# A hybrid four-branch block: RWKV's Gram masks moved to VectorE, and a fourth raw weight buffer in place of a branch slot

## The chip, the cores and the metric

The kernel runs on one core of a Trainium2 chip. The metric is the device time of one execution in microseconds (us), median of several runs; lower is better. The core has TensorE (PE: matmuls, with its weight loads shown apart as PEld), VectorE (DVE), ScalarE (ACT), GpSimd (POOL) and SyncE (SP), which issues DMAs. Each engine works through its own instructions in order and waits on semaphores for the others.

## The reference

The input `x` has 256 tokens of 2048 numbers. It is normalised, multiplied by one wide matrix `w_in` (2048 x 21648), and the columns are split among four branches (HGRN2, S5, RWKV-7, Mamba-2), each 1024 wide. Each branch's output is gated, multiplied by its `w_up`, gated again by a sigmoid of more columns of `w_in`, and summed; then come `w_out`, a norm and the residual:

```python
h = rmsnorm(res, norm_pre[l])
(q_a, f_a, i_a, z_a, u_b, z_b, rkvwa_c, z_c, xbc_d, dt_d, z_d,
 gate_pre) = project_partitioned(h, w_in[l], IN_SPLITS)
...
o_c = rwkv7_branch(...) * jax.nn.silu(z_c)
...
contrib = gate * jnp.einsum('blw,wd->bld', outs[b], w_up[l, b].astype(F32))
merged = contrib if merged is None else merged + contrib
...
y = jnp.einsum('bld,de->ble', merged, w_out[l].astype(F32))
res = res + rmsnorm(y, norm_post[l])
```

The change touches the RWKV branch. Its reference is a recurrence over tokens, with 16 heads of a 64 x 64 state:

```python
sa = jnp.einsum('bhvk,bhk->bhv', state, -kk_t)
state = (state * w_t[:, :, None, :]
         + sa[..., None] * (kk_t * a_t)[:, :, None, :]
         + v_t[..., None] * k_t[:, :, None, :])
return state, jnp.einsum('bhvk,bhk->bhv', state, r_t)
```

The kernel computes it in four chunks of 64 tokens. For every head and chunk it forms Gram matrices between tokens (products of r and kk with k and b), and keeps of each only the causal part: either on and above the diagonal or strictly above it. That is where the masks come in.

## The kernel before

All big weights are streamed from HBM in chunks of 512 KB, 444 of them, each a part of a unit (a block of columns of `w_in`, `w_up`, `w_glu` or `w_out`). The class `_Stream` handles them:

- `load` (L1569) issues a chunk's DMA from SP into a tile `raw`, of which there are `RAW_BUFS` = 3 (L56). `loads` runs ahead of the split by `RAW_BUFS - LAG` chunks in the main loop (L1700). A load into a buffer waits until the split of the chunk that had the buffer before has read it.
- `split` (L1581) makes of `raw` a rounded `hi` on ScalarE (L207, the helper `act`) and the rest `lo` on VectorE (L216, the helper `tt`), so that fp32 accuracy comes from three fast matmuls (hi by h, hi by the low part of h, lo by h). There are four pairs of `hi` and `lo` (`HL_BUFS`).
- `products` issues these matmuls (L261, the helper `mm`): 24 a chunk with 256 columns, or 12 with 512, into a PSUM tile `pg`.

Between the chunks the planner `run_jobs` (L1559) puts the branches' work: each branch is a generator whose `yield`s divide it into stages. Each operation is booked on a modelled time of its engine (`t_pe`, `t_act`, `t_dve`, `t_sw` for GpSimd). Stages are started, by priority, while neither VectorE's nor ScalarE's booked time is more than `AHEAD` = 3.0 us ahead of PE's, and when the work that a stage needs should be done. The order of all instructions on all engines is thus fixed when the program is built, and it depends on every booked cost and on the free slots. If a unit needs a branch that isn't done, `finish` issues the rest of its stages at once.

The branches' tiles of 4 KB a partition come from a pool of `NSLOT` = 37 slots (L54); a `raw` tile is of the same size. Some stages ask for room first (`wait`, and the S5 branch's look ahead at L1473). Branches also use four PSUM banks `pb` (`bank`), asked for with `wait_banks`. DMAs of the branches (`ld`, `ldx`) go through GpSimd's queue in the main loop, and stores (`st`) through ScalarE's.

The Gram stage of RWKV (`rwkv_branch`, L531 to L580) does this for each chunk c of 64 tokens: twice, for four groups of two heads, 8 matmuls of `bk` by `L1` into two banks; then four copies on ScalarE out of PSUM, each 64 partitions x 512, two into `L1[c][e]` (L548) and two into `GB[c]` (L549). After both halves, four `affine_select`s on GpSimd (L561, the helper `select`), each over 64 x 1024 in place, zero the part that isn't causal. Of the two 64 x 64 blocks in each, one keeps the diagonal and the other doesn't; which of them is which alternates with c (o = c % 2). Then `GB`'s strict part is stored to the DRAM tensor `dab` (L562) by GpSimd's queue, and `bk` is transposed and copied into `bkT`. In the profile `L1` shows as `L`. Later the blocks of `dab` are inverted on VectorE, and the recurrence over the four chunks runs on `L1`, `GB`, `bkT`. The S5 branch's tiles (scans at L243 among them) and the evacuations of units run in between.

`setup_consts` makes the constants on GpSimd near the start, among them `lmask` (L356) with memsets and `affine_select`s like those that the change adds.

Of the kernel before, what the change touches and what calls it, by code (L numbers as in the profile page):

```python
# [11 lines left out]
F32 = mybir.dt.float32  # L12
F32R = mybir.dt.float32r
I8 = mybir.dt.int8
BF16 = mybir.dt.bfloat16
AF = mybir.ActivationFunctionType
ALU = mybir.AluOpType
# [33 lines left out]
NPAR = 384  # L51


NSLOT = 37  # L54
SLOT = 1024
RAW_BUFS = 3  # L56
LAG = 1
BANKS = 4
BLOCKED = -1
# [14 lines left out]
class _Kern:  # L74


    def __init__(self, ctx, tc, drams):
# [4 lines left out]
        self.wpool = ctx.enter_context(tc.tile_pool(name="wpool", bufs=3))  # L82
        self.slots = ctx.enter_context(tc.tile_pool(name="slots", bufs=NSLOT))
        self.small = ctx.enter_context(tc.tile_pool(name="small", bufs=1))
# [35 lines left out]
    def room(self, n):  # L120
        return self.live(self.tiles) + n <= NSLOT

# [191 lines left out]
def setup_consts(K):  # L314
    nc = K.nc
    d = K.d
    c = K.const
    K.pt = c.tile([128, NPAR], F32, name="pt")
    src = {"norm_pre": d["norm_pre"], "lb": d["hgrn_lb_logits"], "hgrn_norm": d["hgrn_norm"],
           "s5_d": d["s5_d"], "b_glu": d["s5_b_glu"], "w0": d["rwkv_w0"], "a0": d["rwkv_a0"],  # L320
           "k_k": d["rwkv_k_k"], "k_a": d["rwkv_k_a"], "r_k": d["rwkv_r_k"], "ln_w": d["rwkv_ln_w"],
           "ln_b": d["rwkv_ln_b"], "m2_norm": d["m2_norm"], "conv_b": d["m2_conv_b"],
           "mu": d["rwkv_mu"], "conv_w": d["m2_conv_w"], "a_re": d["s5_a_re"], "a_im": d["s5_a_im"]}
    rows = K.big([128, 3, 128], name="prow")
    nc.vector.memset(rows, 0.0)
    for m, n in enumerate(_PAR_ROWS):
        if m in (6, 12):
            yield
        o, r = PAR[n]
        a = src[n][0]  # L330
        if len(a.shape) == 2:
            a = a.rearrange("a b -> (a b)")
        K.ldx(rows[o % 128:o % 128 + r, o // 128, :], a.rearrange("(r p) -> r p", p=128))
    yield
    K.ones = c.tile([128, 1], F32, name="ones")
    nc.gpsimd.memset(K.ones, 1.0)
    K.halfpi = c.tile([128, 1], F32, name="halfpi")
    nc.gpsimd.memset(K.halfpi, HALF_PI)

    K.ind = c.tile([128, 2, 32], F32, name="ind")  # L340
    nc.gpsimd.memset(K.ind, 0.0)
    for e in range(2):
        for g in range(2):
            nc.gpsimd.memset(K.ind[64 * e:64 * e + 64, g, 2 * g + e:2 * g + e + 1], 1.0)
    K.m64 = c.tile([128, 512], BF16, name="m64")
    nc.gpsimd.memset(K.m64, 1.0)
    nc.gpsimd.memset(K.m64[:, 0:512:64], 0.0)
    K.m256 = c.tile([128, 512], BF16, name="m256")
    nc.gpsimd.memset(K.m256, 1.0)
    nc.gpsimd.memset(K.m256[:, 0:512:256], 0.0)  # L350
    K.causal = c.tile([128, 128], F32, name="causal")
    nc.gpsimd.memset(K.causal, 1.0)
    nc.gpsimd.affine_select(out=K.causal, in_=K.causal, pattern=[[1, 128]], base=0, channel_multiplier=-1,
                            compare_op=ALU.is_ge, fill=0.0)

    K.lmask = c.tile([128, 7, 64], I8, name="lmask")  # L356
    nc.gpsimd.memset(K.lmask, 0.0)
    for e in range(2):
        x = slice(64 * e, 64 * e + 64)
        for lv in range(6):  # L360
            h = 1 << lv
            nb = 32 // h
            v = K.lmask[x, lv + 1, :].rearrange("p (b u) -> p b u", u=2 * h)[:, :, h:2 * h]
            nc.gpsimd.memset(v, 1.0)
            nc.gpsimd.affine_select(out=v, in_=v, pattern=[[-2 * h, nb], [0, h]], base=0, channel_multiplier=1,
                                    compare_op=ALU.is_ge, fill=0.0)
            nc.gpsimd.affine_select(out=v, in_=v, pattern=[[2 * h, nb], [0, h]], base=h - 1, channel_multiplier=-1,
                                    compare_op=ALU.is_ge, fill=0.0)
    K.omu = c.tile([128, 25], F32, name="omu")
    yield  # L370
    for e in range(2):
        x = slice(64 * e, 64 * e + 64)
        nc.vector.tensor_copy(out=K.lmask[x, 0, :], in_=K.ident[x, x])
    yield from K.wait_banks(1)
    ps = K.bank()
    for j in range(3):
        K.tr(ps[:, j * 128:(j + 1) * 128], rows[:, j, :])
    nc.vector.tensor_copy(out=K.pt, in_=ps[:, 0:NPAR])
    K.ts(K.omu, K.parv("mu"), -1.0, 1.0, ALU.mult, ALU.add)
# [16 lines left out]
def rwkv_branch(K, rw):  # L396

    nc = K.nc
# [10 lines left out]
    for g in range(2):  # L409
# [3 lines left out]
        for ii in range(4):  # L413
            i = 4 * g + ii
# [3 lines left out]
        for ii in range(4):  # L418
            i = 4 * g + ii
# [23 lines left out]
    ps = K.bank()  # L443
# [34 lines left out]
    ps = K.bank()  # L478
# [4 lines left out]
    b = ic  # L483
# [10 lines left out]
    L1 = [[K.big([128, 8, 2, 64], name=f"L1{c}{e}") for e in range(2)] for c in range(4)]  # L494
    for c in range(4):
        o = c % 2
        s0, s1 = 64 * c, 64 * c + 64
        for e in range(2):
            x = slice(64 * e, 64 * e + 64)
# [12 lines left out]
    for c in range(4):  # L512
# [3 lines left out]
        for e in range(2):  # L516
            x = slice(64 * e, 64 * e + 64)
# [9 lines left out]
    GB, bkT = [], []  # L527
# [3 lines left out]
    for c in range(4):  # L531
        o = c % 2
        GB.append(K.big([128, 8, 2, 64], name=f"GB{c}"))
        bkT.append(K.big([128, 16, 64], name=f"bkT{c}") if c < 3 else None)
        for i4 in range(2):
            yield from K.wait_banks(2)
            ps = [K.bank([128, 4, 128]) for _ in range(2)]
            for ii in range(4):
                i = 4 * i4 + ii
                for e in range(2):  # L540
                    x = slice(64 * e, 64 * e + 64)
                    K.mm(ps[e][:, ii, :], fl2(bk[c][x, i]), fl2(L1[c][e][x, i]))
            yield 1
            for e in range(2):
                x = slice(64 * e, 64 * e + 64)
                y = slice(64 * (1 - e), 64 * (1 - e) + 64)
                i0 = slice(4 * i4, 4 * i4 + 4)
                K.act(L1[c][e][y, i0].rearrange("p i a b -> p i (a b)"), ps[e][y], AF.Copy)  # L548
                K.act(GB[c][x, i0].rearrange("p i a b -> p i (a b)"), ps[e][x], AF.Copy)  # L549
                if e == 0:  # L550
                    yield 0
            del ps
            if i4 == 0:
                yield 0
        pat = [[0, 8], [-1 if o == 0 else 1, 2], [1, 64]]
        base = 0 if o == 0 else -1
        for e in range(2):
            x = slice(64 * e, 64 * e + 64)
            y = slice(64 * (1 - e), 64 * (1 - e) + 64)
            for ap in (GB[c][x], L1[c][e][y]):  # L560
                K.select(ap, pattern=pat, base=base, channel_multiplier=-1, compare_op=ALU.is_ge, fill=0.0)  # L561
            K.ld(dab[c, :, e, :, :].rearrange("i s t -> s i t"), GB[c][x, :, 1 - o, :])  # L562
        if c == 3:
            bk[c] = None
            break

        pt = []
        yield from K.wait_banks(2)
        for e in range(2):
            x = slice(64 * e, 64 * e + 64)  # L570
            ps = K.bank([128, 8, 64])
            pt.append(ps)
            for i in range(8):
                K.tr(ps[:, i, :], fl2(bk[c][x, i]), 64 * e)
        yield 1
        for e in range(2):
            K.act(bkT[c][:, e:16:2, :], pt[e], AF.Copy)
        bk[c] = None
        del pt, ps
        yield 0  # L580
# [10 lines left out]
    for s in range(31):  # L591
        n, m = s + 1, 31 - s
# [29 lines left out]
    for q in range(2):  # L622
        ps = [K.bank([128, 8, 32]) for _ in range(2)]
        zps.append(ps)
        for o in range(2):
            z0 = 64 * (1 - o) + 32
            for h in range(16):
                i, e = h // 2, h % 2
                x = slice(64 * e, 64 * e + 32)
# [12 lines left out]
    for q in range(2):  # L642
        ps = K.bank([128, 16, 32])
# [44 lines left out]
    for q in range(2):  # L688
# [4 lines left out]
        else:  # L693
            for e in range(2):
                x = slice(64 * e, 64 * e + 64)
# [6 lines left out]
        for o in range(2):  # L702
            c = 2 * q + o
# [4 lines left out]
            for h in range(16):  # L708
                i, e = h // 2, h % 2
# [11 lines left out]
            for h in range(16):  # L721
                i, e = h // 2, h % 2
                K.mm(pu[64 * e:64 * e + 64, i, :], TT[q][ab:ab + 64, h, :], R1(e)[:, i, :])
            yield 1
            for e in range(2):
                x = slice(64 * e, 64 * e + 64)
# [3 lines left out]
            if c < 3:  # L730
                yield from K.wait_banks(1)
                pst = K.bank([128, 8, 64])
                for h in range(16):
                    i, e = h // 2, h % 2
                    K.mm(pst[64 * e:64 * e + 64, i, :], bkT[c][:, h, :], wc[e][:, i, 1, :])
            for h in range(16):
                i, e = h // 2, h % 2
                x = slice(64 * e, 64 * e + 64)
# [3 lines left out]
            if c < 3:  # L742
                if o == 1:
                    carry = GB[0][:, :, 0, :]
                for e in range(2):
                    x = slice(64 * e, 64 * e + 64)
# [16 lines left out]
    v = K.fm("v")  # L763
# [3 lines left out]
    for q in range(2):  # L767
        y = Y[q]
# [15 lines left out]
        for g in range(2):  # L784
            yield from K.wait_banks(1)
            ps = K.bank([128, 4, 128])
            for ii in range(4):
                i = 4 * g + ii
                K.tr(ps[:, ii, :], yf[:, i * 128:(i + 1) * 128])
            yield 1  # L790
            for ii in range(4):
                i = 4 * g + ii
# [713 lines left out]
class _Stream:  # L1506
# [62 lines left out]
    def load(self, j):  # L1569
        u, c = self.chunks[j]  # L1570
        K = self.K
        t = K.wpool.tile([128, u.kc, u.nc_], F32, tag="raw", name=f"raw{j}", bufs=RAW_BUFS)
        k0 = c * u.kc * 128
        K.t_sp = max(K.t_sp, self.split_end.pop(j - RAW_BUFS, 0.0))
        soft, K.soft = K.soft, False
# [99 lines left out]
    def prepare(self):  # L1675
# [3 lines left out]
        self.loaded = -1  # L1679
        self.loads(RAW_BUFS)  # L1680

# [4 lines left out]
    def begin(self, j):  # L1686

        self.step = -HL_BUFS
        self.split(j)
        self.loads(j + 1 + RAW_BUFS)  # L1690

# [603 lines left out]
```

## Time and profile before

| | |
|---|---|
| median of 3 runs | 1429.35 us (1428.59 to 1433.24) |
| the profiled execution | 1436.64 us |
| its span, first to last instruction | 1434.9 us |
| moved by DMA | 287.57 MB, mean 200 GB/s |
| raw weight loads | 444 of 512 KB, all from SP |

Times in the trace are microseconds from the start of the span. A group's row reads: line, engine, operation, output <- inputs, shape, count; then busy time, mean duration of one in ns; then the idle time of the engine just before them, and what ended it. A row of windows gives, for each engine, the busy time within the window and the number of instructions, then the granted TensorE clock (1.00 is full speed), the mean busy share of the DMA engines and GB/s. Busy times of matmuls overlap and their ends are modelled, so a busy PE isn't necessarily PE at its peak. The lines themselves stand in the prediction, each beside what it carries.

### The profile page before, as it was taken

How to read it: one execution, taken by the hardware profiler on the slowest of the kernel's cores; microseconds unless marked ns; L12 is line 12 of the kernel's file. 1: busy time of each engine (PE TensorE's matmuls, PEld its weight loads, DVE VectorE, ACT ScalarE, POOL GpSimd, SP SyncE). 2: the span in 40 equal slices, each digit the busy share in tenths (PEclk: the TensorE clock that was granted, in tenths of full speed). 3: DMA queues.
4: the chain of work that ended last, by engine and by line, in shares of the span. 5: the costliest groups of instructions: out<-in, count | busy, mean ns of one | idle time of the engine just before them, and what ended most of it. 6: DMA issues, size and time to landing. Idle time of an engine off the chain costs nothing.

```text
span 1434.9 us, 24425 instructions
## 1 busy us (share of the span) xinstructions
PE 1391.9 (97%) x9623; PEld 1227.7 (86%) x9623; DVE 1059.2 (74%) x1454; ACT 818.6 (57%) x1129; POOL 157.9 (11%) x267
## 2 busy tenths in 40 slices
PE   8998999988999999899999999999999999999997
PEld 7998998988999878798888888887889888888886
DVE  6775976768965757678988779867876798766654
ACT  5465445565437574466357875678647454554442
POOL 6012004133030102100010000000010100000000
PEclk9999999999999999899999999999999999999999
DMA  7775777676797957966678655656585876686564
GB/s 214 210 232 166 217 219 227 184 168 180 227 240 184 223 178 195 238 202 219 194 231 199 190 184 185 202 182 199 178 191 166 205 218 197 195 271 195 182 195 136
DMA packets 198769, 287.57 MB, mean 200 GB/s; under 512 B 12438, under 2 KB 116735, under 8 KB 198655
## 3 DMA queue, kind: packets, MB, share of 16 engines
q1 hardware_dynamic: 169614, 237.15, 54.6%
q0 software_dynamic: 24944, 42.01, 13.9%
q10 hardware_dynamic: 4096, 6.86, 1.4%
q8 instruction: 75, 1.23, 0.4%
q14 instruction: 40, 0.32, 0.1%
HBM read 267.81 MB, written 18.14 MB: 199 GB/s over the span
## 4 chain that ended last, share of the span: by engine, by line
PE 75%; DMA 9%; DVE 6%; ACT 5%; issue 3%; POOL 1%; ACTq 0%; DVEq 0%; POOLq 0%
PE pg L261 68%; PE pb L261 6%; DMA raw<-in_w_in_dram 6%; DVE lo L216 2%; ACT hi L207 2%; PE pb L267 1%; DMA raw<-in_w_up_dram 1%; DMA hp<-in_m_a_log_dram 1%; DMA bc<-dinv 1%; DVE tb L243 1%; ACT hT L207 0%; DVE ta L216 0%; ACT W L207 0%; DMA ds5c<-cT 0%; DVE ev L229 0%
## 5 line engine op out<-in xcount | busy, mean ns | idle before, releaser
L216 DVE TENSOR_TENSOR lo<-raw,hi 128x1024 fp32r<-128x1024 f32 x444 | 538.9, 1218 | 337.1 <-ACT hi L207 333.1
L207 ACT ACTIVATE hi<-raw 128x1024 fp32r<-128x1024 f32 x444 | 465.6, 1054 | 539.4 <-PE pg L261 284.7
L261 PE MATMUL pg<-h,hi 128*128 128x256 f32 x2624 | 488.5, 289 | 7.2 <-ACT hi L207 6.8
L261 PE MATMUL pg<-hi,h 128*128 128x512 f32 x1408 | 449.3, 393 | 0.0
L261 PEld LDWEIGHTS pg<-h,hi 128*128 128x128 f32 x2624 | 416.4, 195 | 13.8 <-ACT hi L207 7.4
L261 PE MATMUL pg<-h,lo 128*128 128x256 f32 x1312 | 375.9, 288 | 4.8 <-DVE lo L216 2.8
L261 PEld LDWEIGHTS pg<-hi,h 128*128 128x128 f32 x1408 | 264.3, 188 | 59.3 <-issue 3.3
L261 PE MATMUL pg<-lo,h 128*128 128x512 f32 x704 | 274.3, 390 | 0.0
L261 PEld LDWEIGHTS pg<-h,lo 128*128 128x128 f32 x1312 | 255.3, 195 | 6.3 <-DVE lo L216 4.3
L261 PE MATMUL pg<-hi,o 128*128 128x512 f32 x512 | 162.5, 392 | 0.0
L261 PEld LDWEIGHTS pg<-lo,h 128*128 128x128 f32 x704 | 132.3, 188 | 25.8
L261 PEld LDWEIGHTS pg<-hi,o 128*128 128x128 f32 x512 | 96.1, 188 | 21.0 <-issue 1.2
L261 PE MATMUL pg<-lo,o 128*128 128x512 f32 x256 | 99.9, 390 | 0.7 <-DVE lo L216 0.7
L261 PE MATMUL pg<-hi,mhl 128*128 128x512 f32 x224 | 71.1, 391 | 0.0
L207 ACT ACT_TABLE_LOAD x49 | 62.9, 1283 | 4.2 <-DVE mss L235 1.4
L280 POOL DMA_DIRECT2D gb<-in_gate_bias_dram x16 | 8.8, 548 | 507.8 <-DVE gate L216 507.8
L261 PEld LDWEIGHTS pg<-lo,o 128*128 128x128 f32 x256 | 48.1, 188 | 10.5 <-DVE lo L216 1.1
L261 PEld LDWEIGHTS pg<-hi,mhl 128*128 128x128 f32 x224 | 42.0, 188 | 8.6
L243 DVE TENSOR_TENSOR_SCAN tb<-s5p,ta 128x256 f32<-128x256 f32 x64 | 43.9, 732 | 0.1
L261 PE MATMUL pg<-lo,mhl 128*128 128x512 f32 x112 | 43.6, 389 | 0.0
L216 DVE TENSOR_TENSOR ta<-ta,tb 128x512 f32<-128x512 f32 x64 | 41.3, 686 | 0.6
L261 PEld LDWEIGHTS pg<-lo,mhl 128*128 128x128 f32 x112 | 21.0, 188 | 4.3
(367 smaller groups left out, 1326.1 us busy)
## 6 DMA issues: line engine op xcount, KB each, us to landing
raw<-in_w_in_dram SPq DMA_DIRECT2D x340, 512.0 KB
raw<-in_w_up_dram SPq DMA_DIRECT2D x64, 512.0 KB
raw<-in_w_out_dram SPq DMA_DIRECT2D x32, 512.0 KB
us<-duhl POOLq DMA_DIRECT2D x16, 256.0 KB, 8.7
bs<-ds5b POOLq DMA_DIRECT2D x16, 256.0 KB, 10.3
gb<-in_gate_bias_dram POOLq DMA_DIRECT2D x16, 256.0 KB, 5.2
raw<-in_s_w_glu_dram SPq DMA_DIRECT2D x8, 512.0 KB
x<-in_x_dram SPq DMA_DIRECT2D x4, 512.0 KB
```

The costliest lines, as they stand in the source:

```text
L207: return self.nc.scalar.activation(out=out, in_=in_, func=func, **kw)
L216: return self.nc.vector.tensor_tensor(out=out, in0=in0, in1=in1, op=op)
L243: return self.nc.vector.tensor_tensor_scan(out=out, data0=data0, data1=data1, initial=0.0, op0=ALU.mult, op1=ALU.add)
L261: return self.nc.tensor.matmul(out, lhsT, rhs, start=start, stop=stop, **kw)
L267: return self.nc.tensor.transpose(out, in_, self.ident[b:b + p, b:b + p])
L280: return self.nc.gpsimd.dma_start(out=out, in_=in_)
```

## The change

The copies on ScalarE and the selects on GpSimd are replaced by one VectorE operation for each copy: a bitwise AND of the PSUM tile, read as int32, with a constant mask `gmask` of all ones or zeros, written as int32 into `L1` or `GB`. `gmask` has three 64 x 64 blocks: strict, with the diagonal, strict; a slice of two neighbouring blocks serves even and odd chunks. It is made once, on GpSimd, in `setup_consts`. And one slot of the branch pool becomes a fourth `raw` buffer; `loads` and `load` follow `RAW_BUFS`, so loads are issued one chunk further ahead, and four instead of three before the first split.

```diff
-NSLOT = 37
+NSLOT = 36
 SLOT = 1024
-RAW_BUFS = 3
+RAW_BUFS = 4
...
+    K.gmask = c.tile([128, 3, 64], I32, name="gmask")
+    nc.gpsimd.memset(K.gmask, -1)
+    for e in range(2):
+        for n in range(3):
+            v = K.gmask[64 * e:64 * e + 64, n, :]
+            nc.gpsimd.affine_select(out=v, in_=v, pattern=[[1, 64]], base=-1 if n != 1 else 0, channel_multiplier=-1,
                                     compare_op=ALU.is_ge, fill=0.0)
...
-                K.act(L1[c][e][y, i0].rearrange("p i a b -> p i (a b)"), ps[e][y], AF.Copy)
-                K.act(GB[c][x, i0].rearrange("p i a b -> p i (a b)"), ps[e][x], AF.Copy)
+                keep = lambda z: K.gmask[z, 1 - o:3 - o, :].unsqueeze(1).to_broadcast([64, 4, 2, 64])
+                for out, z in ((L1[c][e], y), (GB[c], x)):
+                    K.tt(out[z, i0].bitcast(I32), ps[e][z].rearrange("p i (a b) -> p i a b", a=2).bitcast(I32), keep(z),
+                         ALU.bitwise_and)
...
-        pat = [[0, 8], [-1 if o == 0 else 1, 2], [1, 64]]
-        base = 0 if o == 0 else -1
         for e in range(2):
             x = slice(64 * e, 64 * e + 64)
-            y = slice(64 * (1 - e), 64 * (1 - e) + 64)
-            for ap in (GB[c][x], L1[c][e][y]):
-                K.select(ap, pattern=pat, base=base, channel_multiplier=-1, compare_op=ALU.is_ge, fill=0.0)
             K.ld(dab[c, :, e, :, :].rearrange("i s t -> s i t"), GB[c][x, :, 1 - o, :])
```

More of the change, by code (lines that the diff above doesn't have):

```diff
@@ L14 @@
 I8 = mybir.dt.int8
+I32 = mybir.dt.int32
 BF16 = mybir.dt.bfloat16
@@ L368, in setup_consts @@
                                     compare_op=ALU.is_ge, fill=0.0)
+    K.gmask = c.tile([128, 3, 64], I32, name="gmask")
[4 more added lines that the diff above has]
+            nc.gpsimd.affine_select(out=v, in_=v, pattern=[[1, 64]], base=-1 if n != 1 else 0, channel_multiplier=-1,
+                                    compare_op=ALU.is_ge, fill=0.0)
     K.omu = c.tile([128, 25], F32, name="omu")
```

## The prediction

> **What bounds the kernel now.** I read the page's busy shares first, then the clock of the core, then windows of busy time over the whole span.
>
> ```profile
> span 1434.9 us, 24425 instructions
> PE 1391.9 (97%) x9623; PEld 1227.7 (86%) x9623; DVE 1059.2 (74%) x1454; ACT 818.6 (57%) x1129; POOL 157.9 (11%) x267
> core 0: 1434.9 us, clock 0.984
> sum 600.00, PE 568.62 PEld 534.08 DVE 424.53 ACT 327.88 POOL 124.86; mean PE 9.48 PEld 8.90 DVE 7.08 ACT 5.46 POOL 2.08
> sum 834.90, PE 823.30 PEld 693.63 DVE 634.69 ACT 490.70 POOL 33.04; mean PE 19.60 PEld 16.52 DVE 15.11 ACT 11.68 POOL 0.79
> 1420.00:1434.90 14.90, 6.67 (x30) 5.19 (x28) 7.75 (x18) 1.78 (x6) 0.00 (x0) 0.85 0.39 141
> ```
>
> TensorE sets the pace. The change removes no matmul, so it can win only where PE stands still or runs slowly. The two sums are the first 600 us and the rest. PE is idle 600.00 - 568.62 = 31.4 us in the first, where RWKV runs, and 834.90 - 823.30 = 11.6 us in the second, of which 14.90 - 6.67 = 8.2 us is the kernel's tail, which the change does not touch. A mean clock of 0.984 costs another 0.016 x 1434.9 = 23 us. So the room is some 31 + 23 us at most, less the start of the kernel.
>
> Next, the timeline of PE: its longest idle times after the start, in brackets with what ended them, and windows of 5 us around four of them (columns: PE, PEld, DVE, ACT, POOL busy, granted clock, DMA share, GB/s).
>
> ```profile
> 139.65 0.50 PE L261 MATMUL pg<-h,hi 128*128 128x256 f32 x2 [3.62 <-ACT hi L207]
> 250.38 1.94 PE L267 MATMUL pb<-ident,cx 128*128 128x128 f32 x8 [3.49 <-ACT mrow L207]
> 305.33 0.99 PE L261 MATMUL pb<-us,bs 128*128 128x256 f32 x4 [2.68 <-ACT bkT L207]
> 329.81 1.08 PE L261 MATMUL pb<-ta,cu 128*32 128x256 f32 x8 [4.02 <-ACT bkT L207]
> 593.46 0.50 PE L261 MATMUL pg<-h,hi 128*128 128x256 f32 x2 [2.67 <-ACT hi L207]
> 140.00:145.00 5.00, 4.24 (x21) 4.09 (x20) 3.94 (x8) 2.34 (x3) 2.33 (x4) 0.51 1.06 368
> 145.00:150.00 5.00, 5.00 (x37) 5.00 (x37) 5.00 (x9) 2.27 (x4) 0.00 (x0) 0.81 0.57 161
> 305.00:310.00 5.00, 4.24 (x30) 3.77 (x30) 2.36 (x3) 4.96 (x9) 0.00 (x0) 1.00 0.51 162
> 325.00:330.00 5.00, 0.98 (x19) 0.79 (x20) 5.00 (x9) 2.53 (x4) 0.00 (x0) 0.78 0.43 130
> 330.00:335.00 5.00, 5.00 (x29) 4.19 (x24) 2.33 (x4) 4.35 (x8) 0.00 (x0) 0.54 0.97 276
> 590.00:595.00 5.00, 1.57 (x10) 1.16 (x9) 1.56 (x2) 1.06 (x1) 0.00 (x0) 0.90 1.90 217
> 595.00:600.00 5.00, 4.79 (x22) 4.49 (x22) 3.35 (x5) 3.56 (x5) 0.54 (x1) 0.50 1.02 266
> 600.00:605.00 5.00, 3.36 (x16) 3.40 (x17) 3.85 (x5) 2.94 (x3) 0.00 (x0) 0.50 0.57 176
> 605.00:610.00 5.00, 5.00 (x34) 5.00 (x33) 4.93 (x6) 4.97 (x11) 0.00 (x0) 0.73 0.53 155
> ```
>
> The reader is to see that such an idle time has a second price: the clock granted afterwards. After the stop at 139 us it costs (1 - 0.51) x 5 + (1 - 0.81) x 5 = 3.4 us, after the one at 329 us (1 - 0.78) x 5 + (1 - 0.54) x 5 = 3.4 us, around 593 us 0.5 + 2.5 + 2.5 + 1.35 = 6.9 us. After the 2.68 us at 305 us it costs nothing (clock 1.00).
>
> Then the waits of ScalarE and of SP's DMA queue.
>
> ```profile
> SPq L287 <- DVE lo L216: 934.5, 360, 10.8
> ACT hi L207 <- DMA raw<-in_w_in_dram: 162.9, 80, 9.6
> 138.54 1.06 ACT L207 ACTIVATE hi<-raw 128x1024 fp32r<-128x1024 f32 x1 [9.60 <-DMA raw<-in_w_in_dram]
> 298.90 1.06 ACT L207 ACTIVATE hi<-raw 128x1024 fp32r<-128x1024 f32 x1 [2.61 <-DMA raw<-in_w_in_dram]
> 325.62 1.06 ACT L207 ACTIVATE hi<-raw 128x1024 fp32r<-128x1024 f32 x1 [5.71 <-DMA raw<-in_w_in_dram]
> 592.35 1.06 ACT L207 ACTIVATE hi<-raw 128x1024 fp32r<-128x1024 f32 x1 [5.78 <-DMA raw<-in_w_in_dram]
> 127.36 0.37 SPq L287 DMA_DIRECT2D raw<-in_w_in_dram  x1
> 14.75 2.87 PE pg L261 x24
> ```
>
> SP nearly always waits for one thing, the `lo` that frees a raw buffer. Four of PE's stops have a late raw weight shortly before them, all but the one at 250 us. At 127.36 us a load is issued into a DMA system that the branches' own transfers keep busy (DMA share 1.06 at 140), and the split that needs it starts at 138.54, 11.2 us later. The chain's row gives what one chunk is worth to PE: 24 matmuls, 2.87 us.
>
> **The fourth raw buffer.** Load j then waits for the split of chunk j-4, not j-3, and is written one chunk further ahead in the program; no DMA is added but one load in the first microseconds. Before a burst one more chunk already lies in SBUF. At 139 us that is 2.87 us of PE work laid into 3.62 us; some 0.75 us are left, less than the 2.68 us that left the clock alone, so the 3.4 us go too: **-6.3**. Around 593 us the burst is longer (DMA share 1.90). I take one chunk, 2.87, and one 3.4 of the clock's 6.9: **-6.3**. At 305 us PE waits for ACT copies that queue behind a `hi` held up by raw for 2.61 us at 298.90; a load one chunk earlier covers that: **-2.7**. The start, where one load more is in flight early, I cost at 0: none of PE's long stops after the first matmuls lies there.
>
> The clock rule deserves a doubt. The Trainium skill (TensorE: Matmul & The Clock Gate, What's actually happening) has the clock halved after an idle window of about 3.4 us. The trace agrees at 139 (3.62), 250 (3.49), 305 (2.68, none) and 329 (4.02), and disagrees at 593, where 2.67 us with shorter gaps before it was enough. By that rule alone the remainder at 593 would cost no clock, and the sum would be 3.4 us lower, some 1414 us.
>
> **The masks.** Rows of the groups that go, and the nearest ones to what comes.
>
> ```profile
> L207 ACT ACTIVATE GB<-pb 64x512 f32<-64x512 f32 x24 | 13.8, 590 | 2.6 <-PE pb L261 1.7 <-PE pg L261 0.7
> L207 ACT ACTIVATE L<-pb 64x512 f32<-64x512 f32 x16 | 9.4, 586 | 0.6 <-ACT ev L207 0.4
> L275 POOL TENSOR_SCALAR_AFFINE_SELECT L<-L 64x1024 f32<-64x1024 f32 x8 | 10.2, 1270 | 0.5
> L275 POOL TENSOR_SCALAR_AFFINE_SELECT GB<-GB 64x1024 f32<-64x1024 f32 x8 | 9.5, 1191 | 38.7 <-ACT GB L207 38.7
> L216 DVE TENSOR_TENSOR GB<-pb,W x2: 676/686/695, 504.2 to 505.6; 64x512 f32<-64x512 f32 x2
> L252 DVE COPY_PREDICATED accd<-lmask,pb 128x512 f32<-128x512 int8 x14 | 10.2, 731 | 0.0
> L234 DVE TENSOR_SCALAR ph<-ph 128x512 f32<-128x512 f32 x16 | 7.6, 478 | 0.0
> 236.00:346.00 110.00, 98.78 (x839) 94.67 (x839) 75.06 (x104) 71.52 (x107) 36.38 (x43) 0.94 0.69 182
> 313.38 6.34 DVE L243 TENSOR_TENSOR_SCAN tb<-s5p,ta 128x256 f32<-128x256 f32 x4
> 314.43 1.43 POOL L275 TENSOR_SCALAR_AFFINE_SELECT L<-L 64x1024 f32<-64x1024 f32 x1
> 575.88 1.27 DVE L243 TENSOR_TENSOR_SCAN tb<-s5p,ta 128x256 f32<-128x256 f32 x2
> L365 POOL TENSOR_SCALAR_AFFINE_SELECT lmask<-lmask 64x32 int8<-64x32 int8 x12 | 6.3, 528 | 0.8
> ```
>
> Off ScalarE: 4 chunks x 2 halves x 4 copies = 32 (all 16 of L, 16 of the 24 of GB) x 0.59 = 18.9 us. Off GpSimd: 10.2 + 9.5 = 19.7 us. Onto VectorE: 32 x 0.686 = 22.0 us, the row of the same shape out of PSUM with one SBUF operand. No row shows an AND on int32; by the nearest rows it lies between 32 x 0.478 = 15.3 and 32 x 0.731 = 23.4 us; I take 22.0. Against that, VectorE gets back what the selects took: four scans last 6.34 us while selects run beside them (one of 1.43 us at 314.43), and two last 1.27 us without, so 6.34 - 2.54 = 3.8 us in that place alone. The net is +18 us: VectorE goes from 75 to about 93 of the 110 us between 236 and 346, 85%. None of this is on PE's path by itself. The ANDs come in pairs of 1.4 us, and what queues behind a pair on VectorE is the next `lo`, which PE's chunk and, with it, SP's next load wait for. The cover is PE's reserve of split chunks, four `hi`/`lo` pairs. If it is gone, each pair costs PE up to 1.4 us.
>
> The stop at 329.81 (4.02 + 3.4 = 7.4 us) sits behind the slowed scans and a raw load that VectorE's late `lo` released late. Scans 3.8 us shorter and a buffer more speak for all of it going, 8 ANDs of 0.686 = 5.5 us on the same engine against it: I take half, **-3.7**. The DMA `dab<-GB` moves only from behind selects to behind ANDs. The new constant is a memset and six selects on GpSimd before the RWKV stage; six by the mean of the last row, of half their size, are 3.2 us, and at most six of the large select's 1.27 us, 7.6 us, beside PE's start, with GpSimd's S5 loads behind them: 0, unless one of these is late.
>
> **What is new.** Every booked cost moves, the planner lays the stages after 234 us anew, and the slot pool loses one of 37. The stop at 250 us (a load of `cn` through GpSimd's queue) is of that sort and may stay, move or double. I allow one new stop of its size: 3.49 + 3.4 = **+6.9**; from 0 to two of them is open.
>
> **Sum**: -6.3 - 6.3 - 2.7 - 3.7 + 6.9 = -12.1 us. The profiled execution took 1436.64 us (span 1434.9 and 1.7 around it), which is 7.3 us above the median of the runs, 1429.35; the same difference off the median gives 1417.
>
> **Rivals.**
> *All the stops but one go.* No new stop, all of the 329 us one (-7.4) and all of the clock at 593 (-9.8 in place of -6.3): -6.3 - 9.8 - 2.7 - 7.4 = -26, 1403 us. For it: four of the five stops have a late raw before them. Against it: the burst at 593 lasts longer than a chunk. The Trainium skill (DMA: Bandwidth & Descriptors, Queues, rings and completion order) says that a DMA engine takes turns between queues packet by packet, so a fourth load in SP's one queue would not win a larger share in a burst; only its head start would count, which leaves 593 at one chunk and speaks against this rival. No row here shows the turns.
> *The buffer only shortens.* The stops at 139 and 593 lose a chunk each but the clock still falls, the one at 305 goes, the one at 329 stays because ANDs take the scans' gain, and a new stop comes: -2.9 - 2.9 - 2.7 + 6.9 = -1.6, 1428 us: no change. For it: 593 shows that gaps under 3 us can cost clock.
> *VectorE becomes the bound of the mask stage (slower).* At 85% on average, a `lo` stands behind ANDs, conv and S5 work in every mask chunk, and each of the other three chunks gets a stop like 329's: 3 x 7.4 = +22, against -12.6 at 139 and 593: +10, 1439 us. It decides once VectorE's queue ahead of a `lo` outlasts PE's reserve; between 310 and 330 us it already did once. For it: that stop. Against: the planner starts no job stage when VectorE's booked time runs 3 us ahead of PE's, and ANDs are booked there.
>
> **How the numbers follow.** Forecast 1417: 0.45; 1403: 0.20; 1428: 0.20; 1439: 0.15. A measurement can tell about 0.3%, 4.3 us, from no change. Faster: most of the forecast, the first rival and a little of the second: 0.66. Same: most of the second: 0.19. Slower: 0.15. For 8 in 10 the range runs from 1402, the first rival's time, to 1436, into the slower one. The forecast's own range is 1409 to 1424.
>
> **What would show it.** Right: PE's idle time at 139 us under 2 us and the clock there at 1.00; the group `hi` waiting for raw far below 162.9 us; scans near 0.64 us each; DVE some 18 us up, ACT 19 and POOL 18 down; mean clock above 0.984. Wrong: ANDs well over 0.73 us; the same stops with the clock at 0.5 after them (the buffer only shortens); new idle times of PE between 236 and 346 us released by `lo` (VectorE bound); PE waiting in the second part, where today it does not.

## The result

The changed kernel takes 1407.31 us (median of 4 runs, 1405.5 to 1410.55) against 1430.81 us for the kernel before: a ratio of 0.9838, 95% interval [0.981, 0.9865], or 23.5 us less. The forecast was 12 us less, 1417 us.

The page of the changed kernel, then its mean clock, then its two parts in windows (columns as before):

```profile
span 1406.8 us, 24394 instructions
PE 1381.4 (98%) x9623; PEld 1217.7 (87%) x9623; DVE 1069.4 (76%) x1486; ACT 805.5 (57%) x1100; POOL 140.5 (10%) x258
```

```profile
core 0: 1406.8 us, clock 0.995
```

```profile
0.00:600.00 600.00, 585.30 (x5167) 552.04 (x5168) 456.93 (x756) 329.09 (x486) 105.43 (x199) 0.99 0.78 215
600.00:1406.80 806.80, 796.10 (x4458) 665.70 (x4457) 612.44 (x731) 476.38 (x615) 35.06 (x59) 1.00 0.67 196
```

Nearly all of it came where the prediction looked for it. PE's idle time in the first 600 us fell from 31.4 to 14.7 us. PE's busy time over the span, for the same 9623 matmuls, fell from 1391.9 to 1381.4 us, while the mean clock rose from 0.984 to 0.995. That is 16.7 + 10.5 = 27.2 of the 28.1 us between the two spans (1434.9 and 1406.8); the profiled execution of the kernel before was one of its slower ones, so the medians lie closer together. PE's stops behind the start, from its timeline: what is left at 132 us of the one at 139, then the longest:

```profile
132.22 0.50 PE L262 MATMUL pg<-h,hi 128*128 128x256 f32 x2 [0.31 <-ACT hi L208]
159.54 1.07 PE L268 MATMUL pb<-ident,cx 128*128 128x128 f32 x8 [1.66 <-DVE cx L236]
257.18 0.39 PE L262 MATMUL pg<-h,lo 128*128 128x256 f32 x1 [2.42 <-DVE lo L217]
435.23 0.25 PE L262 MATMUL pb<-T,GB 32*32 32x32 f32 x3 [2.22 <-issue]
872.51 1.14 PE L262 MATMUL pb<-ta,cu 128*32 128x256 f32 x8 [1.70 <-DVE ta L217]
```

The groups that are new and the scans of S5 over the whole kernel, then ScalarE's wait for raw weights:

```profile
L217 DVE TENSOR_TENSOR GB<-pb,gmask 64x512 int32<-64x512 int32 x16 | 11.0, 689 | 0.2
L217 DVE TENSOR_TENSOR L<-pb,gmask 64x512 int32<-64x512 int32 x16 | 10.9, 684 | 0.2
L244 DVE TENSOR_TENSOR_SCAN tb<-s5p,ta 128x256 f32<-128x256 f32 x64 | 40.1, 674 | 0.2
```

```profile
ACT hi L208 <- DMA raw<-in_w_in_dram: 85.1, 39, 5.2
```

An AND lasts 0.69 us, as the row of the same shape said, and the wait for raw weights of `w_in` has halved from 162.9 us. Which half of the change did it, the profile doesn't say: buffer, masks and a new order of all stages came together. The experiments take them apart.

### The profile page after: what moved, and what is told of

Read it like the earlier page. It is cut to its first block, busy times and chain, and to the rows that moved or that the text cites. A ratio compares the mean times of both kernels' runs of the same rounds, so it can differ in the third digit from the quotient of the medians.

```text
span 1406.8 us, 24394 instructions
## 1 busy us (share of the span) xinstructions
PE 1381.4 (98%) x9623; PEld 1217.7 (87%) x9623; DVE 1069.4 (76%) x1486; ACT 805.5 (57%) x1100; POOL 140.5 (10%) x258
## 4 chain that ended last, share of the span: by engine, by line
PE 82%; DVE 6%; DMA 5%; ACT 4%; issue 2%; POOL 0%; ACTq 0%; SPq 0%; DVEq 0%; POOLq 0%
PE pg L262 74%; PE pb L262 7%; DMA raw<-in_w_in_dram 3%; DVE lo L217 3%; ACT hi L208 2%; PE pb L268 1%; DMA bs<-ds5b 1%; ACT hT L208 1%; DMA x<-in_x_dram 1%; DVE ev L230 1%; ACT L208 0%; DVE GB L217 0%; DVE L L217 0%; DVE dk L236 0%; DMA dab<-GB 0%
## 5 line engine op out<-in xcount | busy, mean ns | idle before, releaser
L262 PE MATMUL pg<-h,hi 128*128 128x256 f32 x2624 | 476.5, 284 | 0.3 <-ACT hi L208 0.3
L262 PEld LDWEIGHTS pg<-h,hi 128*128 128x128 f32 x2624 | 407.0, 191 | 5.2 <-issue 2.4
L262 PE MATMUL pg<-h,lo 128*128 128x256 f32 x1312 | 369.9, 284 | 4.0 <-DVE lo L217 3.2
L262 PEld LDWEIGHTS pg<-h,lo 128*128 128x128 f32 x1312 | 249.8, 191 | 5.2 <-DVE lo L217 3.9
L244 DVE TENSOR_TENSOR_SCAN tb<-s5p,ta 128x256 f32<-128x256 f32 x64 | 40.1, 674 | 0.2
```

Of the source, the lines that this page charges most:

```text
L244: return self.nc.vector.tensor_tensor_scan(out=out, data0=data0, data1=data1, initial=0.0, op0=ALU.mult, op1=ALU.add)
L262: return self.nc.tensor.matmul(out, lhsT, rhs, start=start, stop=stop, **kw)
```

## The experiments

Three theories: **BUFFER** (the fourth raw buffer), **MASKS** (the copies and selects gone from ScalarE and GpSimd), **ORDER** (the planner's new order). Times are medians; ratios are to the kernel before, run on the same chip (its medians were 1429.39, 1431.57 and 1433.14 us in the three sets). A ratio is the one on record with its 95% interval, not the quotient of the two medians; in the first set the two differ (the first run below has 0.9846 on record, its medians give 0.9866).

### The buffer alone, the order kept

```diff
-        self.slots = ctx.enter_context(tc.tile_pool(name="slots", bufs=NSLOT))
+        self.slots = ctx.enter_context(tc.tile_pool(name="slots", bufs=36))
...
-        t = K.wpool.tile([128, u.kc, u.nc_], F32, tag="raw", name=f"raw{j}", bufs=RAW_BUFS)
+        t = K.wpool.tile([128, u.kc, u.nc_], F32, tag="raw", name=f"raw{j}", bufs=4)
```

The planner still counts 3 and 37, so every engine gets the instructions of the kernel before in the same order; only what a load must wait for differs.

> The kernel before with its masks on ScalarE and GpSimd and its order of instructions on every engine kept, but four raw buffers and 36 slots. Theory BUFFER (the fourth raw buffer alone brings most of the 23 us, by shortening PE's waits for weights): 1408 to 1416 us, the stops at 139 and 593 us gone or under 1 us. Theory MASKS (taking the copies from ScalarE and the selects from GpSimd brings it): 1426 to 1431 us. Theory ORDER (the planner's new order brings it): 1426 to 1431 us, the stops stay.

Measured: 1410.17 us, ratio 0.9846 [0.9805, 0.9887]. BUFFER as expected; MASKS and ORDER were not even in the kernel. Windows around three stops show what became of the clock. First the kernel before, then this one:

```profile
120.00:150.00 30.00, 24.87 (x181) 24.24 (x180) 17.18 (x27) 10.59 (x15) 10.29 (x17) 0.89 0.75 207
230.00:260.00 30.00, 26.51 (x221) 24.97 (x219) 17.18 (x26) 18.04 (x28) 12.53 (x17) 0.89 0.68 199
560.00:610.00 50.00, 43.47 (x288) 38.62 (x287) 30.08 (x36) 23.94 (x33) 11.72 (x20) 0.86 1.10 240
```

```profile
120.00:150.00 30.00, 27.25 (x223) 25.90 (x221) 21.52 (x36) 14.27 (x18) 10.29 (x17) 1.00 0.81 238
230.00:260.00 30.00, 29.66 (x261) 29.03 (x260) 22.63 (x38) 18.90 (x26) 8.53 (x12) 1.00 0.70 203
560.00:610.00 50.00, 47.44 (x371) 45.95 (x370) 36.32 (x40) 31.18 (x43) 6.65 (x10) 0.97 0.99 254
```

The same stretch of time holds other work in the two runs, so the gain is sized in another way. PE executes the same 9623 matmuls in the same order in both, and one and the same matmul can be looked up in both timelines; by how much it starts earlier here is what has been gained up to it:

| stretch, up to the matmul that starts at | before, us | here, us | gained within, us |
|---|---|---|---|
| the start, to ahead of the stop at 139 us | 135.76 | 131.92 | 3.84 |
| the stop at 139 us and its clock | 160.04 | 152.58 | 3.62 |
| no stop | 246.02 | 238.56 | 0.00 |
| the stop at 250 us and its clock | 262.02 | 248.84 | 5.72 |
| no stop | 299.96 | 286.78 | 0.00 |
| the stop at 305 us | 306.16 | 291.44 | 1.54 |
| the stop at 329 us and its clock | 336.64 | 321.30 | 0.62 |
| small gaps | 579.90 | 564.03 | 0.53 |
| the stops around 593 us and their clock | 612.05 | 587.62 | 8.56 |
| the rest, to the end of the span | 1434.9 | 1408.0 | 2.4 |

These are two single executions, 26.9 us apart.

The stop at 250 us is the instructive one, for no weight ends it: PE waits there for `cx`, made of `cn`, which GpSimd's queue loads. The prediction's row names ScalarE's `mrow` as what ended it, but with the fourth buffer the same matmuls start before `mrow` is done, and in both runs they start some 0.15 us after `cx` is done. ScalarE's, GpSimd's, PE's and VectorE's timelines ahead of it, in the kernel before:

```profile
226.87 1.06 ACT L207 ACTIVATE hi<-raw 128x1024 fp32r<-128x1024 f32 x1 [4.15 <-DMA raw<-in_w_in_dram]
231.25 1.06 ACT L207 ACTIVATE hi<-raw 128x1024 fp32r<-128x1024 f32 x1 [3.32 <-DMA raw<-in_w_in_dram]
232.21 0.58 ACT L207 ACTIVATE uhl<-pg 128x512 fp32r<-128x512 f32 x1
233.09 1.37 POOL L280 DMA_DIRECT2D duhl<-uhl  x2 [6.23 <-ACT uhl L207]
238.66 1.16 PE L261 MATMUL pb<-L,bk 64*128 64x128 f32 x16
239.24 0.93 POOL L280 DMA_DIRECT2D cn<-in_s_c_im_dram  x1
248.40 1.83 DVE L235 TENSOR_SCALAR cx<-cn,s5pm 128x512 f32<-128x512 f32 x2 [4.57 <-DMA cn<-in_s_c_im_dram]
```

And the same with the fourth buffer, GpSimd's and PE's timelines:

```profile
222.54 1.37 POOL L280 DMA_DIRECT2D duhl<-uhl  x2 [4.11 <-ACT uhl L207]
228.92 0.93 POOL L280 DMA_DIRECT2D cn<-in_s_c_im_dram  x1
231.21 1.16 PE L261 MATMUL pb<-L,bk 64*128 64x128 f32 x16
239.78 1.07 PE L267 MATMUL pb<-ident,cx 128*128 128x128 f32 x8 [0.34 <-DVE cx L235]
```

A late raw weight holds ScalarE, in order, at a `hi`; the copy `uhl` behind it is late; GpSimd's queue, in order too, waits with its store; and the load of `cn` behind that starts 0.6 us after PE's second Gram block instead of 2.3 us before it. PE then stands 0.34 us instead of 3.49. The late weight costs PE through three queues, though what PE waits for there is no weight.

What the buffer leaves, PE's rows in this run:

```profile
290.61 0.99 PE L261 MATMUL pb<-us,bs 128*128 128x256 f32 x4 [1.13 <-ACT bkT L207]
315.09 0.85 PE L261 MATMUL pb<-ta,cu 128*32 128x256 f32 x8 [4.02 <-ACT bkT L207]
578.48 1.09 PE L267 MATMUL pb<-ident,Y 128*128 128x128 f32 x4 [2.56 <-DVE Y L216]
```

### The masks alone, the order kept

```diff
+    def keep_as_copy(self, out, in0, in1):
+        self.book("t_act", 0.06 + self._n(out) * 0.87e-3, out, (in0,))
+        return self.nc.vector.tensor_tensor(out=out, in0=in0, in1=in1, op=ALU.bitwise_and)
...
+                    K.keep_as_copy(out[z, i0].bitcast(I32), ...)
...
+            for ap in (GB[c][x], L1[c][e][y]):
+                K.book("t_sw", 0.07 + K._n(ap) * 1.05e-3, ap, (ap,))
```

`RAW_BUFS` is 3 and `NSLOT` 37; the ANDs are booked as the copies and selects were, so they stand where the copies stood.

> ANDs on VectorE in the order of the kernel before, with three raw buffers and 37 slots: the masks alone. BUFFER: 1426 to 1434 us. MASKS: 1424 or less. VECTOR BOUND: 1435 or more.

Measured: 1432.24 us, ratio 1.0 [0.9978, 1.0023]. Nothing, either way. Its profiled execution was the slowest of its twelve (1439.92 us). The page shows the work moved all the same:

```profile
PE 1390.3 (97%) x9623; PEld 1226.5 (85%) x9623; DVE 1072.8 (75%) x1486; ACT 800.3 (56%) x1097; POOL 140.3 (10%) x258
```

VectorE is up by 13.6 us (22.0 of ANDs, less 8.4 got back), ScalarE down by 18.3, GpSimd by 17.6.

### Both, the order kept

The masks as above, with `bufs=4` and `bufs=36` as in the first run.

> Four raw buffers and ANDs on VectorE, but the order of the kernel before kept on every engine (the ANDs stand where the copies stood). Against the run with the buffer alone in that order, 1410. BUFFER (masks are worth next to nothing by themselves): 1406 to 1414 us. MASKS (they pay once weights are no longer late, through the scans and the stop of 4.02 us at 315): 1404 or less. VECTOR BOUND (ANDs in front of lo cost more than they free): 1415 or more.

Measured: 1408.35 us, ratio 0.9836 [0.9805, 0.9867]. 1.8 us below the buffer alone, within the intervals. In one and the same order the four corners are 1.0, 0.9846, 1.0 and 0.9836: the buffer is the change.

### Orders

The buffer with the plan laid anew for it:

```diff
-NSLOT = 37
+NSLOT = 36
...
-RAW_BUFS = 3
+RAW_BUFS = 4
```

> The buffer and the slot alone, the plan laid anew for them, masks as before. BUFFER: within 4 us of the run with the order kept, 1408 to 1416. MASKS: 1426 to 1431. ORDER: over 5 us from the run with the order kept, to either side.

Measured: 1419.03 us, ratio 0.9911 [0.9881, 0.9942], 9 us above the same buffers and slots in the old order, and outside the 1408 to 1416 us of BUFFER: ORDER counts here, and it costs. The same order with ANDs in place of copies and selects, booked as those:

> The whole change, but the ANDs are booked like the copies and selects that they replace, so the order of all stages is that of the run with the buffer alone; only the engine of the masks differs from it. BUFFER: within 4 us of that run. MASKS: 10 us or more below it. ORDER: within 4 us of that run, and 5 us or more from the changed kernel's 1407.

Measured: 1423.11 us, ratio 0.9948 [0.9923, 0.9972]. That is 4 us above the same order with copies and selects: the masks gain nothing here either. And the changed kernel in its own order with the fourth raw buffer left unused (`bufs=3`, three loads before the first split, 36 slots):

> The changed kernel in its own order and with its ANDs, but three raw buffers (the fourth is left unused, the slots stay 36). BUFFER: 1422 us or more. MASKS: 1412 us or less. ORDER: 1412 us or less.

Measured: 1445.16 us, ratio 1.0073 [1.0046, 1.0101], slower than the kernel before. ORDER thus has an effect, but no gain: with three buffers the new order is worse than the old (1.0073 against 1.0), with four it is level (0.9838 against 0.9836). PE's timeline in the run with three buffers has stops at 677 and 900 us that the old order doesn't have, and the wait of `hi` for raw is back:

```profile
677.22 2.07 PE L262 MATMUL pb<-xst,cbt 128*128 128x256 f32 x4 [3.72 <-DVE xst L217]
900.01 1.58 PE L262 MATMUL pb<-ta,cu 128*32 128x256 f32 x8 [3.10 <-DVE ta L217]
```

```profile
ACT hi L208 <- DMA raw<-in_w_in_dram: 194.4, 88, 8.4
```

In the run with ANDs booked as copies, PE waits where the plan thinks an AND is done on ScalarE:

```profile
280.74 0.77 PE L266 MATMUL pb<-L,bk 64*128 64x128 f32 x2 [3.41 <-DVE GB L224]
```

That the wrong booking makes this order slow isn't shown by it. The same order with the copies on ScalarE, rightly booked, has stops of 2.77 and 2.37 us in that stage, at 278 and 297 us, and the same wrong booking in the old order cost nothing (0.9836).

### What the selects cost

The changed kernel with the selects put back behind its ANDs, not booked, so that all else keeps its order:

```diff
+            for ap in (GB[c][x], L1[c][e][y]):
+                nc.gpsimd.affine_select(out=ap, in_=ap, pattern=[[0, 8], [-1 if o == 0 else 1, 2], [1, 64]], ...)
             K.ld(dab[c, :, e, :, :].rearrange("i s t -> s i t"), GB[c][x, :, 1 - o, :])
```

> The changed kernel with the 16 selects of the kernel before added behind its ANDs on GpSimd, where they alter no value; the order of all else is kept. PORT (selects take time from VectorE's scans and lo, and delay dab, and that matters to PE): 1411 us or more, scans slower again. NO PORT (VectorE's loss is hidden): within 3 us of 1407, scans slower or not.

Measured: 1415.78 us, ratio 0.9885 [0.9853, 0.9916], 8 us more than the changed kernel. Timelines of GpSimd, VectorE and PE in this run:

```profile
366.49 1.18 POOL L570 TENSOR_SCALAR_AFFINE_SELECT GB<-GB 64x1024 f32<-64x1024 f32 x1
364.93 3.29 DVE L217 TENSOR_TENSOR ta<-ta,tb 128x512 f32<-128x512 f32 x2
372.49 2.17 POOL L281 DMA_DIRECT2D XA<-dab  x2 [1.39 <-DMA dab<-GB]
384.54 0.19 DVE L217 TENSOR_TENSOR invtmp<-XT,XA 128x31 f32<-128x31 f32 x1 [9.04 <-DMA XA<-dab]
389.23 0.58 PE L262 MATMUL pg<-h,lo 128*128 128x256 f32 x1 [4.20 <-DVE lo L217]
```

The same places in the changed kernel:

```profile
360.15 1.29 DVE L217 TENSOR_TENSOR ta<-ta,tb 128x512 f32<-128x512 f32 x2
363.82 2.17 POOL L281 DMA_DIRECT2D XA<-dab  x2 [1.54 <-PE pg L262]
374.03 0.19 DVE L217 TENSOR_TENSOR invtmp<-XT,XA 128x31 f32<-128x31 f32 x1 [4.44 <-DMA XA<-dab]
```

Two costs appear at once. Beside a select, two operations of VectorE last 3.29 us instead of 1.29. And `XA` is loaded 8.7 us later (4.8 of them are a delay that the stage had before: its last AND, too, comes 4.8 us later), so VectorE, in order, stands 9.04 us at the inversion's first step, `lo` waits behind it, and PE stops for 4.20 us. To tell them apart, the selects work on a scratch tile behind the `dab` stores, where nothing waits for them, with 35 slots to make room for it:

```diff
+def scratch_selects(K):
+    for e in range(2):
+        for h in range(2):
+            ap = K.scratch[64 * (e ^ h):64 * (e ^ h) + 64]
+            K.nc.gpsimd.affine_select(out=ap, in_=ap, ...)
...
+        scratch_selects(K)
```

> The changed kernel in its own order with 35 slots, and with 16 selects of the old size on a scratch tile that nothing waits for, behind the dab stores of each chunk (behind the loads of XA in the last). The run with the selects in the path gave 1415.8. LATENCY (those 8 us came from dab and XA arriving later, with lo queued behind the waiting VectorE): within 3 us of 1407. PORT (they came from VectorE's operations being slowed beside selects): 1411 us or more.

Measured: 1407.86 us, ratio 0.9828 [0.9798, 0.9859]: LATENCY, by the total. The page has the other cost still in it, and so have VectorE's and PE's timelines beside the selects:

```profile
PE 1379.7 (98%) x9623; PEld 1217.3 (87%) x9623; DVE 1077.6 (77%) x1486; ACT 806.2 (57%) x1100; POOL 167.3 (12%) x275
```

```profile
330.92 6.93 POOL L411 TENSOR_SCALAR_AFFINE_SELECT scratch<-scratch 64x1024 f32<-64x1024 f32 x4
330.43 2.21 DVE L230 SCALAR_TENSOR_TENSOR ph<-ph 128x512 f32<-128x512 f32 x1
335.92 2.56 PE L262 MATMUL pb<-L,bk 64*128 64x128 f32 x16 [2.49 <-ACT bkT L208]
```

The same operation and the same matmuls in the changed kernel:

```profile
330.72 0.69 DVE L230 SCALAR_TENSOR_TENSOR ph<-ph 128x512 f32<-128x512 f32 x1
334.70 1.64 PE L262 MATMUL pb<-L,bk 64*128 64x128 f32 x16 [0.61 <-ACT bkT L208]
```

VectorE loses 1077.6 - 1069.4 = 8.2 us to the selects, and here PE does notice: `ph` is late, ScalarE waits for it with `bkT` behind, and PE stops. By the starts of the same matmuls, PE falls 4.8 us behind the changed kernel between 331 and 346 us; with the selects in the path it falls 5.4 us behind there, and 5.8 us more at the stop behind `XA`. Only the second loss is gone in the run with the scratch tile. That its total is level all the same comes from elsewhere: its trace gains 3.2 us around 257 us, where the changed kernel has a stop, and some 6 us behind 436 and around 872 us, which the run with the selects in the path gains too. So the loss through late results is shown. Whether the slowed operations of VectorE cost device time by themselves stays open: the total says no, this stretch says yes.

### More buffers

The changed kernel's order with `bufs=5` for raw and 35 slots:

> The changed kernel in its own order with five raw buffers and 35 slots: the suspected gain once more. If some of PE's remaining 2.42 us stop at 257 us and the starts of DMA bursts still wait for weights: 1400 to 1404 us. If the fourth buffer already covers all bursts: 1405 to 1409. If fewer slots hold the branches up: 1410 or more.

Measured: 1400.41 us, ratio 0.9776 [0.9744, 0.9808]. Five buffers and 35 slots in the old order, with the old masks and then with the ANDs:

> The kernel before in its own order, masks on ScalarE and GpSimd, with five raw buffers and 35 slots. BUFFER goes on: 1400 to 1405 us, and the masks aren't needed for it. If the stops left at 290 to 315 us and 578 us come from the branches and not from weights: 1406 to 1410.

Measured: 1403.82 us, ratio 0.9796 [0.9769, 0.9822].

> ANDs on VectorE in the order of the kernel before, five raw buffers, 35 slots. If the ANDs are worth nothing by themselves: within 3 us of the run with five buffers and the old masks. If they pay once weights are no longer late: 4 us or more below it.

Measured: 1402.21 us, ratio 0.9784 [0.9758, 0.981]. Again 1.6 us between them: the masks aren't needed. The two were measured on one chip, and their times hardly overlap (1402.4 to 1405.5 us and 1401.5 to 1403.0), so here the ANDs do seem to be worth some 0.1%. Six buffers and 34 slots in the changed kernel's order:

> The changed kernel in its own order with six raw buffers and 34 slots. With five its splits waited 11.1 us in all for weights, so the gain is used up: 1398 to 1402 us; 1405 or more if the branches now wait for slots.

Measured: 1397.57 us, ratio 0.9752 [0.9723, 0.9781], the fastest, a little under what was expected; its interval lies below that of the changed kernel. ScalarE's wait for raw with six buffers:

```profile
ACT hi L208 <- DMA raw<-in_w_in_dram: 10.0, 4, 4.0
```

In this order it went 194.4 (three buffers), 85.1 (four), 11.1 (five) and 10.0 us (six). With that the way of a deeper queue is at its end; what the last buffer gained, 3 us by the medians, is inside the intervals.

## Why the prediction came out as it did

**Right.** The bound and the room: PE's stops in the first 600 us and the clock behind them. The mechanism of the first term: the stop at 139 us went, and the clock stayed at full speed behind it. The cost of an AND: 0.686 us forecast, 0.684 to 0.689 measured; VectorE's net load, +18 forecast, came to +13.6, because the selects had taken 8.4 us in all where the prediction counted 3.8 in one place (in the changed kernel's own order the sum of all is +10.2). The slower rival, that the ANDs bind PE, did not come: the masks alone give 1.0. Its sign, a new stop between 236 and 346 us released by `lo`, did come once in the changed kernel, at 257 us, but no AND stands ahead of that `lo`. VectorE itself had stood still, for a `hi` that ScalarE held back while it waited for `hp`, a small load of the Mamba-2 branch through GpSimd's queue:

```profile
247.78 0.20 ACT L208 ACTIVATE hp<-hp 16x1 f32<-16x1 f32 x1 [6.66 <-DMA hp<-in_m_a_log_dram]
250.34 1.22 DVE L217 TENSOR_TENSOR lo<-raw,hi 128x1024 fp32r<-128x1024 f32 x1 [8.20 <-ACT hi L208]
```

**Mis-sized.** The gain was twice the sum. With the buffer alone, in the old order, the terms measured:

- At 139 us: -6.3, but 3.6 us. The stop went; what is left is a wait of 1.18 us for a `lo` just behind it, at 140.70 us of that run. The clock's price was also set too high, here and below: (1 - clock) x 5 us counts time in which PE stood anyway. Between 325 and 330 us, charged with 1.1 us, PE was busy for 0.98 us.
- Around 593 us: one chunk and half of the clock, -6.3. It measured 8.6 us, nearer to the -9.8 that the first rival had.
- The stop at 250 us: "all but the one at 250 us" have a late raw behind them, and it was counted as the planner's kind that stays. That reading was wrong. It hangs on the raw weight too, through ScalarE's and GpSimd's queues, and was worth 5.7 us. The step that failed was to ask only what ended PE's wait, and not why the load of `cn` was issued late.
- The new stop, +6.9: with four buffers the new order cost nothing against the old one. The caution was not baseless: with three buffers the same order costs 0.7%, and the plan laid anew for the buffer alone lost 9 us.
- The start, 0: 3.8 us ahead of the stop at 139 us, in small steps.
- Small gaps elsewhere, not in the sum: 2.9 us.

**Wrong in its cause.** The -3.7 at 329 us was given to shorter scans and a load released earlier. With the buffer alone that stop stays at 4.02 us. With ANDs too, in the old order, it is shorter with four buffers, but not with five:

```profile
314.68 0.64 PE L266 MATMUL pb<-ta,cu 128*32 128x256 f32 x8 [2.65 <-ACT bkT L208]
312.10 1.08 PE L266 MATMUL pb<-ta,cu 128*32 128x256 f32 x8 [4.18 <-ACT bkT L208]
```

In none of the three runs does ScalarE wait for a raw weight between 280 and 316 us. So neither the ANDs nor earlier loads remove it, and the late raw weight ahead of it in the kernel before was not what held it. It is absent where the plan was laid anew and the Gram stage stands elsewhere, as in the changed kernel. The -2.7 at 305 us measured 1.5 (2.68 to 1.13 us).

**The rivals.** The first (all stops but one go, 1403) lies closest to the measured 1407, though not through the masks. The Trainium skill's round of the queues (DMA: Bandwidth & Descriptors, Queues, rings and completion order) was held against it: only a head start, no larger share. No run here measures shares, so whether the loads gained more than a head start stays open; a fifth buffer still gained and brought the waits from 85.1 to 11.1 us. The Trainium skill's clock rule (TensorE: Matmul & The Clock Gate, What's actually happening) held at 257 us of the changed kernel, where 2.42 us idle left the clock at 1.00, and not at 435 us, where 2.22 us among 32 x 32 matmuls went with a clock of 0.66:

```profile
260.00:265.00 5.00, 5.00 (x44) 5.00 (x43) 4.90 (x9) 2.46 (x3) 0.00 (x0) 1.00 0.66 191
435.00:440.00 5.00, 4.77 (x31) 4.53 (x31) 1.37 (x2) 2.58 (x9) 0.52 (x1) 0.66 0.90 302
```

**What stays open.** Why the changed kernel's order is worse with three buffers and level with four was not taken apart stage by stage, nor why the order planned for the buffer alone is 9 us slower than the old one. The masks may be worth the 1.6 to 1.8 us by which the medians differ in two pairs of runs; the pair on one chip speaks for it, and the intervals against the kernel before can't tell. Whether VectorE's slowing beside selects costs device time is open too.

## What to carry to other kernels

When the bound engine stands still, follow the wait back through every in-order queue, not only to its last releaser: one late weight on ScalarE can reach TensorE through GpSimd's DMA queue. A buffer more for the stream that feeds the bound engine can be worth more than work taken off engines that are not on its path; test the two halves of a change apart and in one fixed order of instructions, since a new order alone moved this kernel by up to 1.1% (0.9948 against 0.9836, both with four buffers and ANDs). Work on a side engine hurts by when its result arrives, rather than by its busy time; what it slows on a neighbouring engine has to be followed to the bound engine too.

## What the runs showed that was not expected

Selects that nothing waits for took 8.2 us of VectorE's time, and PE stood for 2.49 us behind them in one place, and yet the total was level; the same number in the path of one DMA cost 8 us. And a plan that books an operation on the wrong engine need not be slower: with ANDs and four buffers, ANDs booked on ScalarE and GpSimd took 1423.11 us in the order planned for four buffers, but 1408.35 in the one planned for three, and the plan that books them on VectorE took 1407.31.
